# Quarter sums of the Strassen weights on VectorE, and one PSUM copy on ScalarE, in a decoder-trunk step

## The chip, the core and the metric

One Trainium2 (trn2) core runs the whole kernel as one launch. The metric is the device time of one execution in microseconds (us); three runs of the kernel before the change gave 1285.36, 1286.39 and 1287.26 us, so its median is 1286.39 us. Engines are named as in the profile: PE is TensorE's matmul, PEld its weight load, DVE is VectorE, ACT is ScalarE, POOL is GpSimd, SP is SyncE, which issues the loads.

## The reference

One inference step of a two-layer trunk, in fp32: 512 prompt tokens and 64 sample tokens (8 sequences of 8), model width 1024. Layer 0 is a gated recurrent block, layer 1 a sliding-window attention, and each is followed by a SwiGLU feed-forward block (FFN). The FFN is the part that the change touches:

```python
D_MODEL = 1024; D_FF = 2816; DEPTH = 2

def swiglu(h, w_in, w_out):
    gate, up = jnp.split(h @ w_in, 2, axis=-1)
    return (jax.nn.silu(gate) * up) @ w_out

for l in range(DEPTH):
    ...
    h = modulate(rms_norm(x, norm_g[l, 1]), sh2, sc2)
    x = x + g2[:, None, :] * swiglu(h, ffn_w_in[l], ffn_w_out[l])
```

`w_in` is 1024 x 5632 and `w_out` 2816 x 1024 in each layer.

## The kernel before

**Tiling.** The tokens stand in two halves, h = 0 and 1, of 288 columns (256 prompt and 32 sample tokens). A weight tile is 128 output columns deep over the contracted rows. To keep fp32 accuracy every operand is split into a high part (a cast to fp32r, on ACT) and a low part (the remainder, a subtraction on DVE), and a product is three matmuls of 128 x 288 per 128 rows: high by high, high by low, low by high.

**The FFN.** The first three of the 22 column tiles of each FFN are done plainly. For each of the other 19 (i = 3 to 21) the gate tile and the up tile (each 1024 x 128, loaded into a `raw` buffer of 128 x 1024) and the two token halves are taken as a 2 x 2 by 2 x 2 block product, and Strassen's form (Winograd's variant) does it with seven products of 512 rows instead of eight. A product is 12 matmuls, seven are 84. The weight operands are quarters of the gate and up tile, 128 x 512 each: r11 and r12 in the gate's buffer, r21 and r22 in the up's. The seven are called `11`, `12`, `22`, `S1`, `S2`, `S3`, `S4`: three plain quarters and four that need sums. S1 = r21 + r22; S2 needs two subtractions (r21 becomes r11 - r21, then r11 becomes r22 - r11, which is S2; the new r21 is S3); S4 = r12 - r11. All are written in place into the `raw` buffers, so each tile has four sums of 128 x 512 in fp32, 152 over both layers. `operand` (line 1204) then casts the quarter to high on ACT and subtracts on DVE for low, into a `wh` buffer; 10 `wh` and 4 `raw` buffers are shared by all weights.

**PSUM.** The seven products of a tile go to three PSUM banks (function `seven`): bank a takes `11` then `12`, bank e takes `S1` then `S4`, bank b takes `S2`, then `S3`, then `22`, each on top of what stands there. After S2 DVE adds the saved product `11` into bank b in place (`mm<-mm,ta`), and the finished sum is copied out to SBUF (`u2`, a `td` buffer). Only then may the matmuls of S3 go on in bank b. After S3 DVE adds bank b to the saved S1 product (`td<-mm,td`), and only then may `22` write on. On PE the order is S1, S2, then usually `12` and the next tile's `11`, then S3, S4, `22`.

**What follows.** silu of the gate on ACT, gate times up (on DVE for h = 0, on POOL for h = 1, `td<-td,td`), the split of the result, and after each group of 6, 6, 6 or 4 tiles eight output products of 2 x 18 (or 12) matmuls with the residual add: DVE (`x<-mm,mods,x`) and POOL (`x<-x,ta`, 128 x 32).

**What sets the order.** The code records every instruction with a cost from a small table, and a list scheduler (`schedule`) places them by priority and by the start that its cost table gives. Each engine then runs its own instructions strictly in that order. So moving an operation to another engine can change the order on all engines around it; the order is fixed when the kernel is built. Since all operations are issued from one helper line, the profile's rows carry L447 throughout, and groups are told apart by tile names: `raw` the loaded weights, `wh` split weights, `mm` PSUM banks, `ta`, `tb`, `td`, `sl` SBUF buffers, `h` the split norm output, `x` the residual stream.

The functions that the change touches, with what calls them:

Of the kernel before, what the change touches and what calls it, by code (L numbers as in the profile page):

```python
# [27 lines left out]
HC = 288  # L28
# [445 lines left out]
def trunk_kernel(ctx, tc, a):  # L474
    nc = tc.nc
    rec = Recorder(a["shadow"])
    V, S, G, T, Q = (Engine(rec, n, o) for n, o in (("DVE", nc.vector), ("ACT", nc.scalar), ("POOL", nc.gpsimd), ("PE", nc.tensor), ("SP", nc.sync)))
# [10 lines left out]
    def ps(pool=pmm, tag="mm"):  # L488
        cnt[0] += 1
        return rec.tile(pool, tag, NMM if tag == "mm" else (8 - NMM), RMM if tag == "mm" else 1, [P, 512], F32, f"{tag}{cnt[0]}")  # L490
# [509 lines left out]
    def residual(h, o, c, g, last):  # L1000
        xp, xs = x[h][:, c, 0:HP], v48(x[h][:, c, HP:HC])
        V.scalar_tensor_tensor(xp, o[:, 0:HP], mp(g, c), xp, ALU.mult, ALU.add)
        t = ta()
        V.tensor_tensor(v48(t.f[:, 0:32]), v48(o[:, HP:HC]), msam(g, c, h), ALU.mult)
        (V if g == L1 + G2 and c == KC - 1 else G).tensor_tensor(xs, xs, v48(t.f[:, 0:32]), ALU.add)
        t.done()
        if last and (g != L1 + G2 or c < KC - 1):
            square(h, c)
# [147 lines left out]
    for m in range(KC):  # L1156
# [3 lines left out]
            lambda h, o, m=m: residual(h, o, m, G1, True),  # L1160
# [8 lines left out]
    def ffn(l, g, after):  # L1169
# [34 lines left out]
        def operand(i, name, src, sums=()):  # L1204
            w = W[i, name] = whs()
            for o, p, q, op in sums:
                G.tensor_tensor(o, p, q, op)
            S.copy(w.r[:, 0:H2], src)
            V.tensor_tensor(w.r[:, H2 : 2 * H2], src, w.f[:, 0:H2], ALU.subtract)

        def steps(i):
# [8 lines left out]
            def a11():  # L1220
                operand(i, "11", views()[0])

            def a22():
                operand(i, "22", views()[3])

            def s1():
                r11, r12, r21, r22 = views()
                operand(i, "S1", r22, [(r22, r21, r22, ALU.add)])
# [36 lines left out]
        def pump(want=lambda: True):  # L1265
            while todo and (whs.live + todo[0][0] <= 2 * NHI):
                todo.popleft()[1]()
            assert want()
            load_more()

        def right(name):

            if name in ("T2", "T3", "T4"):
                return [(p.r[:, 0:HC], q.r[:, 0:HC]) for p, q in X2[int(name[1])]]
            h, c0 = {"B11": (0, 0), "B21": (0, 4), "T1": (1, 0), "B22": (1, 4)}[name]
            v = h4r(h)
            return [(v[:, k, 0, :], v[:, k, 1, :]) for k in range(c0, c0 + 4)]
# [3 lines left out]
        def seven(i, name):  # L1281

            pump(lambda: (i, name) in W)
            w = W.pop((i, name))
            bank, ops = {"11": ("a", "B11"), "12": ("a", "B21"), "S1": ("e", "T1"), "S2": ("b", "T2"), "S3": ("b", "T3"),
                         "22": ("b", "T4"), "S4": ("e", "B22")}[name]
            b = B.setdefault(i, {})
            if bank not in b:
                b[bank] = ps()
            o = b[bank][:, 0:HC]  # L1290
            first = name in ("11", "S1", "S2")
            for k, (xh, xl) in enumerate(right(ops)):
                hi, lo = [w.r[:, q + k * P : q + (k + 1) * P] for q in (0, H2)]
                T.matmul(o, hi, xh, start=first and k == 0, stop=False, skip_group_check=True)
                T.matmul(o, hi, xl, start=False, stop=False, skip_group_check=True)
                T.matmul(o, lo, xh, start=False, stop=k == 3, skip_group_check=True)
            w.done()
            pump()
            if name == "11":
                b["p1"] = ta()  # L1300
                S.copy(b["p1"].f[:, 0:HC], o)
            elif name == "S1":
                b["p5"] = td()
                S.copy(b["p5"].f[:, 0:HC], o)
            elif name == "S2":

                V.tensor_tensor(o, o, b["p1"].f[:, 0:HC], ALU.add)
                b["p1"].done()
                b["u2"] = td()
                V.tensor_copy(b["u2"].f[:, 0:HC], o)  # L1310
            elif name == "12":

                b["g"] = ta()
                S.activation(b["g"].f[:, 0:HC], o, AF.Silu)
            elif name == "S3":

                y = b["p5"].f[:, 0:HC]
                V.tensor_tensor(y, o, y, ALU.add)
            elif name == "22":

                y = b["g"].f[:, 0:HC]
                V.tensor_tensor(y, y, o, ALU.mult)
                whole(0, i, b["g"])
                del B[i]
            else:

                y, z = b["u2"].f[:, 0:HC], b["p5"].f[:, 0:HC]
                V.tensor_tensor(y, o, y, ALU.add)
                S.activation(y, y, AF.Silu)
                G.tensor_tensor(z, y, z, ALU.mult)  # L1330
                b["u2"].done()
                whole(1, i, b["p5"])

        def whole(h, f, t):
            m = mid[h][f] = (sl(F32R), sl(F32R))
            split(m[0].r[:, 0:HC], m[1].r[:, 0:HC], t.f[:, 0:HC])
            t.done()
# [20 lines left out]
        def emit():  # L1358
# [4 lines left out]
            for k in range(len(GROUPS)):  # L1363
                if k == 1 and l == 0:
                    sink_setup()
                for i in range(max(PLAIN, n_), n_ + GROUPS[k]):

                    if i == PLAIN:
                        for j, w in ((0, "11"), (1, "11"), (0, "12")):
                            seven(i + j, w)  # L1370
                    seven(i, "S1")
                    seven(i, "S2")
                    if i == PLAIN:
                        seven(i + 1, "12")
                    elif i > PLAIN + 1:
                        seven(i, "12")
                    if i > PLAIN and i + 1 < n_ + GROUPS[k]:
                        seven(i + 1, "11")
                    seven(i, "S3")
                    ada_pace(2)  # L1380
                    seven(i, "S4")
                    seven(i, "22")
# [606 lines left out]
```

## Time and profile before

| What | Value |
|---|---|
| runs | 1285.36, 1286.39, 1287.26 us |
| span of the profiled execution | 1287.3 us |
| PE busy | 1250.5 us (97%), 9532 instructions |
| DVE busy | 913.8 us (71%) |
| ACT busy | 659.3 us (51%) |
| POOL busy | 482.6 us (37%) |
| four quarter sums per tile, POOL | 152 of 128 x 512, mean 1486 and 1460 ns |
| splits of 128 x 512, DVE | 282, mean 883 ns |
| the u2 copy, DVE | 38 of 128 x 288, mean 456 ns |

The profiled execution's span, 1287.3 us, stands 0.9 us above the median of the runs and equals the slowest of them to 0.1 us; the page shows nothing around the span. A group's row reads: line, engine, operation, output <- inputs, shape, count, then total busy us and mean ns of one, then idle time of the engine before them and who ended it. A timeline row reads: start us, length us, engine, operation, number of instructions merged, and in brackets the engine's idle time before it with the releaser. The matmuls on `tb` (they belong to S2, S3 and `22`) run from 279.6 to 634.8 us in layer 0 and from 923.1 to 1244.8 us in layer 1, with output products between the groups.

### The profile page before, as it was taken

Reading aid. Unit: us, or ns where it says so; the run is one execution under the profiler, and the core shown is the slowest. Engines: PE = TensorE matmul, PEld = TensorE weight load, DVE = VectorE, ACT = ScalarE, POOL = GpSimd, SP = SyncE. Lnnn points to the kernel's source line nnn. Section 1 sums busy time; section 2 is a strip of 40 time slices with the busy share of each in tenths; the row PEclk is TensorE's granted clock in tenths of the full one; section 3 lists DMA queues with packets and bytes.
Section 4 is the critical chain, followed back from the end, with each engine's and each line's share of the span. In section 5 each row is a group of like instructions: output and inputs, shape, how many; then the busy total and the mean of one; then the engine's idle time right before and its main releaser. Section 6 shows DMA issues by size and latency. Waiting matters only on the chain.

```text
span 1287.3 us, 25427 instructions
## 1 busy us (share of the span) xinstructions
PE 1250.5 (97%) x9532; PEld 1173.3 (91%) x9532; DVE 913.8 (71%) x2161; ACT 659.3 (51%) x1470; POOL 482.6 (37%) x710
## 2 busy tenths in 40 slices
PE   7999999999999999999989999999999999999997
PEld 5788899898999999999988987899999999999997
DVE  6988785886478457646679787448965875885777
ACT  4789873753245235414466678438533542552433
POOL 3476630142354145324234435110424533642422
PEclk9999999999999999999999999899999999999998
DMA  9956454525456655554342321233241332233232
GB/s 306 326 165 217 151 164 148 169 63 184 135 152 188 192 170 164 164 180 140 107 97 48 60 75 51 68 94 111 75 123 50 99 115 80 69 107 91 67 98 74
DMA packets 223982, 165.40 MB, mean 128 GB/s; under 512 B 23758, under 2 KB 209066, under 8 KB 223827
## 3 DMA queue, kind: packets, MB, share of 16 engines
q1 hardware_dynamic: 223410, 163.45, 42.2%
q8 instruction: 75, 1.23, 0.4%
q14 instruction: 49, 0.39, 0.1%
q0 software_dynamic: 448, 0.32, 0.1%
HBM read 160.85 MB, written 4.87 MB: 129 GB/s over the span
## 4 chain that ended last, share of the span: by engine, by line
PE 76%; DVE 12%; ACT 4%; POOL 3%; issue 2%; DMA 1%; SPq 1%; ACTq 0%; POOLq 0%; DVEq 0%
PE mm L447 72%; PE ada L447 4%; DVE sl L447 4%; DVE wh L447 3%; POOL raw L447 3%; ACT wh L447 1%; DVE ta L447 1%; DVE h L447 1%; DVE td L447 1%; DVE tb L447 1%; ACT ta L447 1%; ACT L447 1%; ACT h L447 1%; SPq L447 1%; DMA wh<-in_ada_w_dram 1%
## 5 line engine op out<-in xcount | busy, mean ns | idle before, releaser
L447 PE MATMUL mm<-h,wh 128*128 128x288 f32 x4128 | 598.7, 299 | 9.2 <-ACT h L447 4.2
L447 PEld LDWEIGHTS mm<-h,wh 128*128 128x128 f32 x4128 | 563.6, 189 | 30.2 <-issue 10.7
L447 PE MATMUL mm<-sl,wh 128*128 128x288 f32 x3218 | 460.5, 296 | 0.8 <-ACT ta L447 0.8
L447 PEld LDWEIGHTS mm<-sl,wh 128*128 128x128 f32 x3218 | 436.6, 188 | 8.6 <-issue 6.7
L447 ACT CAST wh<-raw 128x512 fp32r<-128x512 f32 (+2 forms) x388 | 266.8, 710 | 301.4 <-PE mm L447 221.0
L447 DVE TENSOR_TENSOR wh<-raw,wh 128x512 fp32r<-128x512 f32 (+2 forms) x388 | 358.3, 948 | 50.5 <-ACT wh L447 46.7
L447 DVE SCALAR_TENSOR_TENSOR x<-mm,mods,x 128x256 f32<-128x256 f32 x160 | 77.1, 482 | 153.1 <-PE mm L447 152.9
L447 POOL TENSOR_TENSOR raw<-raw 128x512 f32<-128x512 f32 x76 | 110.9, 1460 | 188.1 <-DVE wh L447 187.5
L447 POOL TENSOR_TENSOR x<-x,ta 128x32 f32<-128x32 f32 x152 | 54.0, 355 | 308.7 <-DVE ta L447 308.5
L447 POOL TENSOR_TENSOR raw<-raw,raw 128x512 f32<-128x512 f32 x76 | 112.8, 1486 | 3.7
L447 PE MATMUL mm<-tb,wh 128*128 128x288 f32 (+1 forms) x488 | 89.6, 299 | 7.9 <-DVE td L447 5.4
L447 PEld LDWEIGHTS mm<-tb,wh 128*128 128x128 f32 x488 | 72.2, 188 | 12.4 <-DVE td L447 8.8
L447 POOL TENSOR_TENSOR td<-td,td 128x288 f32<-128x288 f32 x38 | 31.1, 817 | 113.7 <-ACT td L447 105.1
L447 PE MATMUL mm<-ta,wh 128*128 128x288 f32 (+1 forms) x254 | 56.0, 298 | 0.0
L447 DVE TENSOR_TENSOR td<-mm,td 128x288 f32<-128x288 f32 x76 | 33.4, 452 | 26.8 <-PE mm L447 26.5
L447 ACT ACTIVATE ta<-x 128x288 f32<-128x288 f32 x56 | 24.8, 444 | 50.9 <-POOL x L447 48.0
L447 PE MATMUL ada<-reg,cz 128*32 128x512 f32 (+1 forms) x448 | 50.3, 553 | 0.4 <-DMA reg<-in_ada_w_dram 0.2
L447 DVE TENSOR_TENSOR sl<-ta,sl 128x288 fp32r<-128x288 f32 x54 | 45.7, 849 | 2.2 <-ACT sl L447 2.0
L447 ACT COPY td<-mm 128x256 f32<-128x256 f32 (+1 forms) x102 | 33.8, 353 | 23.9 <-PE mm L447 20.8
L447 ACT ACTIVATE ta<-mm 128x288 f32<-128x288 f32 x54 | 21.4, 411 | 45.4 <-PE mm L447 44.9
L447 PEld LDWEIGHTS mm<-ta,wh 128*128 128x128 f32 x254 | 41.6, 188 | 1.7 <-ACT wh L447 0.8
L447 ACT ACTIVATE ta<-ta,stat 128x256 f32<-128x256 f32 (+2 forms) x72 | 32.3, 471 | 17.8 <-DVE stat L447 17.0
(202 smaller groups left out, 1250.4 us busy)
## 6 DMA issues: line engine op xcount, KB each, us to landing
raw<-in_ffn_w_in_dram SPq DMA_DIRECT2D x88, 512.0 KB
reg<-in_ada_w_dram SPq DMA_DIRECT2D x80, 512.0 KB
raw<-in_ffn_w_out_dram SPq DMA_DIRECT2D x48, 384.0 KB
raw<-in_rnn_w_in_dram SPq DMA_DIRECT2D x16, 512.0 KB
reg<-in_kv_ada_w_dram SPq DMA_DIRECT2D x16, 512.0 KB
wh<-in_ada_w_dram SPq DMA_DIRECT2D x24, 256.0 KB
raw<-in_rnn_w_out_dram SPq DMA_DIRECT2D x8, 512.0 KB
raw<-in_ffn_w_out_dram SPq DMA_DIRECT2D x16, 256.0 KB
```

What stands on the lines that cost most here:

```text
L447: self.rec.add(eng, lambda: getattr(obj, name)(*map(real, args), **{k: real(v) for k, v in kw.items()}), cost, outs, ins, func, lat, port, ...
```

## The change

The four sums of a Strassen tile are issued on DVE instead of POOL, and the copy of u2 out of PSUM is issued on ACT instead of DVE. Nothing else in the code is changed; the computed values are the same.

```diff
         def operand(i, name, src, sums=()):
             w = W[i, name] = whs()
             for o, p, q, op in sums:
-                G.tensor_tensor(o, p, q, op)
+                V.tensor_tensor(o, p, q, op)
             S.copy(w.r[:, 0:H2], src)
             V.tensor_tensor(w.r[:, H2 : 2 * H2], src, w.f[:, 0:H2], ALU.subtract)
...
             elif name == "S2":
                 V.tensor_tensor(o, o, b["p1"].f[:, 0:HC], ALU.add)
                 b["p1"].done()
                 b["u2"] = td()
-                V.tensor_copy(b["u2"].f[:, 0:HC], o)
+                S.copy(b["u2"].f[:, 0:HC], o)
```

The scheduler makes a new order from this. PE keeps its order up to the first Strassen tile, and outside the Strassen tiles; inside them products change places by up to 15 matmuls. Three places, on DVE and ACT.

**DVE, first Strassen tile of layer 0, before** (`wh<-raw` are splits, `mm<-mm,ta` is the add of product `11` into bank b after S2, the COPY is u2, `td<-mm,td` with mm_3940 the add after S3):

```order
L447 TENSOR_TENSOR td_3828<-td_3828,mm_3825 128x288
L447 TENSOR_TENSOR sl_3876<-td_3828,sl_3870 128x288
L447 TENSOR_TENSOR wh_3864<-raw_3400,wh_3864 128x512
L447 TENSOR_TENSOR wh_3880<-raw_3284,wh_3880 128x512
L447 TENSOR_TENSOR wh_3914<-raw_3284,wh_3914 128x512
L447 TENSOR_TENSOR wh_3931<-raw_3755,wh_3931 128x512
L447 TENSOR_TENSOR wh_3947<-raw_3894,wh_3947 128x512
L447 TENSOR_TENSOR mm_3940<-mm_3940,ta_3888 128x288
L447 COPY td_3972<-mm_3940 128x288
L447 TENSOR_TENSOR wh_3961<-raw_3755,wh_3961 128x512
L447 TENSOR_TENSOR td_3943<-mm_3940,td_3943 128x288
```

and the same stretch in the changed kernel (`raw<-raw` are sums):

```order
L447 TENSOR_TENSOR wh_3872<-raw_3755,wh_3872 128x512
L447 TENSOR_TENSOR raw_3755<-raw_3755 128x512
L447 TENSOR_TENSOR raw_3755<-raw_3500,raw_3755 128x512
L447 TENSOR_TENSOR raw_3500<-raw_3755,raw_3500 128x512
L447 TENSOR_TENSOR wh_3915<-raw_3755,wh_3915 128x512
L447 TENSOR_TENSOR raw_3500<-raw_3500 128x512
L447 TENSOR_TENSOR wh_3929<-raw_3500,wh_3929 128x512
L447 TENSOR_TENSOR wh_3936<-raw_3755,wh_3936 128x512
L447 TENSOR_TENSOR wh_3956<-raw_3500,wh_3956 128x512
L447 TENSOR_TENSOR mm_3948<-mm_3948,ta_3894 128x288
L447 TENSOR_TENSOR wh_3972<-raw_3877,wh_3972 128x512
L447 TENSOR_TENSOR wh_3997<-raw_3892,wh_3997 128x512
```

All eight sums of the first two tiles now stand ahead of the add into bank b, between the splits; the copy is gone from this queue. From the split wh_3726, which opens this stretch in both orders, to the add there are 18 instructions of 128 x 512 and two of 128 x 288.

**DVE, middle of a six-tile group of layer 1, before:**

```order
L447 TENSOR_TENSOR mm_13190<-mm_13190,ta_13116 128x288
L447 COPY td_13225<-mm_13190 128x288
L447 TENSOR_TENSOR wh_13215<-raw_12996,wh_13215 128x512
L447 TENSOR_TENSOR wh_13239<-raw_12996,wh_13239 128x512
L447 TENSOR_TENSOR wh_13246<-raw_13006,wh_13246 128x512
L447 TENSOR_TENSOR wh_13261<-raw_12996,wh_13261 128x512
L447 TENSOR_TENSOR wh_13268<-raw_13140,wh_13268 128x512
L447 TENSOR_TENSOR wh_13275<-raw_13148,wh_13275 128x512
L447 TENSOR_TENSOR td_13195<-mm_13190,td_13195 128x288
L447 TENSOR_TENSOR td_13225<-mm_13155,td_13225 128x288
```

and now:

```order
L447 TENSOR_TENSOR mm_13193<-mm_13193,ta_13123 128x288
L447 TENSOR_TENSOR wh_13222<-raw_12992,wh_13222 128x512
L447 TENSOR_TENSOR raw_12968<-raw_12968 128x512
L447 TENSOR_TENSOR wh_13251<-raw_12968,wh_13251 128x512
L447 TENSOR_TENSOR wh_13265<-raw_13106,wh_13265 128x512
L447 TENSOR_TENSOR td_13216<-mm_13193,td_13216 128x288
L447 TENSOR_TENSOR wh_13281<-raw_13130,wh_13281 128x512
L447 TENSOR_TENSOR raw_13130<-raw_13130 128x512
L447 TENSOR_TENSOR td_13234<-mm_13174,td_13234 128x288
L447 TENSOR_TENSOR raw_13130<-raw_13106,raw_13130 128x512
```

Between the add after S2 and the add after S3 (`td<-mm,td`, the first of the two) stood the copy and six splits; now three splits and one sum stand there.

**ACT, the same place, before** (COPY ta is the saved product `11`, ACTIVATE the silus, CAST wh the high parts):

```order
L447 ACTIVATE ta_13235<-mm_13093 128x288
L447 CAST wh_13239<-raw_12996 128x512
L447 CAST wh_13246<-raw_13006 128x512
L447 COPY ta_13254<-mm_13231 128x288
L447 CAST wh_13261<-raw_12996 128x512
```

and now:

```order
L447 COPY td_13216<-mm_13174 128x288
L447 CAST wh_13222<-raw_12992 128x512
L447 COPY td_13234<-mm_13193 128x288
L447 ACTIVATE ta_13242<-mm_13100 128x288
L447 CAST wh_13251<-raw_12968 128x512
L447 COPY ta_13261<-mm_13238 128x288
L447 CAST wh_13265<-raw_13106 128x512
```

The new copy (td_13234) stands behind one cast and ahead of the silu of the gate.

**DVE, first Strassen tile of layer 1, now** (raw_11955 is the first weight load of the third Strassen tile):

```order
L447 TENSOR_TENSOR wh_11969<-raw_11269,wh_11969 128x512
L447 TENSOR_TENSOR raw_11458<-raw_11458 128x512
L447 TENSOR_TENSOR wh_11985<-raw_11458,wh_11985 128x512
L447 TENSOR_TENSOR wh_11993<-raw_11819,wh_11993 128x512
L447 TENSOR_TENSOR wh_12006<-raw_11458,wh_12006 128x512
L447 TENSOR_TENSOR wh_12013<-raw_11955,wh_12013 128x512
L447 TENSOR_TENSOR mm_11987<-mm_11987,ta_11928 128x288
L447 TENSOR_TENSOR wh_12049<-raw_11995,wh_12049 128x512
L447 TENSOR_TENSOR td_12001<-mm_11987,td_12001 128x288
```

Here too all eight sums of two tiles have moved ahead of the add into bank b: from the split wh_11787, which stands at the same place in both orders, to the add there are 19 instructions of 128 x 512 and two of 128 x 288. On PE the product S2 of this tile starts 15 matmuls earlier than before, and 21 matmuls (products `12` and S4) stand between it and S3.

## The prediction

> **What bounds the kernel now.** I read the page first.
>
> ```profile
> span 1287.3 us, 25427 instructions
> PE 1250.5 (97%) x9532; PEld 1173.3 (91%) x9532; DVE 913.8 (71%) x2161; ACT 659.3 (51%) x1470; POOL 482.6 (37%) x710
> PE 76%; DVE 12%; ACT 4%; POOL 3%; issue 2%; DMA 1%; SPq 1%; ACTq 0%; POOLq 0%; DVEq 0%
> ```
>
> PE is the bound, and the change takes nothing from it. So the change can only win what PE loses to waits inside the Strassen tiles, and only lose by making new ones. Next, the stretches (length; PE, PEld, DVE, ACT, POOL busy with counts; clock; DMA share; GB/s), and PE's and PEld's waits for DVE. The last two rows below are the weight loads' waits of the windows 262 to 302 and 1000 to 1235 us.
>
> ```profile
> 262.00:296.50 34.50, 30.80 (x231) 30.32 (x229) 29.11 (x40) 16.90 (x37) 18.77 (x13) 1.00 0.28 85
> 1016.80:1039.90 23.10, 22.94 (x171) 22.48 (x170) 20.11 (x30) 12.51 (x26) 13.73 (x10) 1.00 0.29 81
> 1152.40:1235.00 82.60, 82.60 (x622) 82.42 (x623) 53.87 (x98) 30.88 (x60) 31.99 (x34) 1.00 0.29 84
> PE mm L447 <- DVE td L447: 5.4, 5, 2.6
> PEld mm L447 <- DVE td L447: 4.2, 2, 2.8
> PEld mm L447 <- DVE td L447: 2.8, 9, 0.5
> ```
>
> A matmul of a full stretch takes 82.60/622 = 0.133 us. PE idles 5.4 us for `td`; the weight loads stall longer, because a short wait disappears under the modelled ends of earlier matmuls. They are the better account: 4.2 in layer 0's first two tiles and 2.8 in layer 1's groups. PE's own rows at the places:
>
> ```profile
> 281.19 1.88 PE L447 MATMUL mm<-h,wh 128*128 128x288 f32 x13
> 284.17 1.06 PE L447 MATMUL mm<-tb,wh 128*128 128x288 f32 x6 [1.10 <-DVE td L447]
> 296.48 1.06 PE L447 MATMUL mm<-tb,wh 128*128 128x288 f32 x6 [2.60 <-DVE td L447]
> 297.38 1.35 PE L447 MATMUL mm<-sl,wh 128*128 128x288 f32 x6
> 298.52 2.94 PE L447 MATMUL mm<-h,wh 128*128 128x288 f32 x12
> 301.30 0.56 PE L447 MATMUL mm<-tb,wh 128*128 128x288 f32 x3
> 923.13 0.43 PE L447 MATMUL mm<-tb,wh 128*128 128x288 f32 x2
> 938.87 0.66 PE L447 MATMUL mm<-tb,wh 128*128 128x288 f32 x3 [1.11 <-DVE td L447]
> 1045.97 0.68 PE L447 MATMUL mm<-tb,wh 128*128 128x288 f32 x3 [0.29 <-DVE td L447]
> 297.80:301.20 3.40, 3.40 (x17) 3.40 (x16) 2.44 (x4) 0.00 (x0) 0.00 (x0) 0.51 0.39 116
> ```
>
> The last row is a window: after the 2.60 us wait the granted clock is 0.51. From 297.38 to 301.30, 18 matmuls take 3.92 us instead of 18 x 0.133 = 2.40, so 1.5 us go there. What may be won is therefore 4.2 + 1.5 in layer 0's start, 1.3 at 938.87 (1.11 idle and a late second matmul), and 2.8 in the groups: **9.8 us**, with 5.4 (the visible idle) as the least.
>
> **Why DVE is late there.** DVE and POOL around the longest wait:
>
> ```profile
> 290.23 3.52 DVE L447 TENSOR_TENSOR wh<-raw,wh 128x512 fp32r<-128x512 f32 x2 [0.66 <-ACT wh L447]
> 294.04 1.52 DVE L447 TENSOR_TENSOR sl<-ta,sl 128x288 fp32r<-128x288 f32 x1
> 295.48 0.45 DVE L447 TENSOR_TENSOR mm<-mm,ta 128x288 f32<-128x288 f32 x1
> 295.97 0.46 DVE L447 COPY td<-mm 128x288 f32<-128x288 f32 x1
> 290.21 2.98 POOL L447 TENSOR_TENSOR raw<-raw,raw 128x512 f32<-128x512 f32 x2
> 293.92 1.32 POOL L447 TENSOR_TENSOR raw<-raw 128x512 f32<-128x512 f32 x1 [0.72 <-DVE wh L447]
> ```
>
> Two splits take 3.52 us while POOL runs sums, and a small split takes 1.52 while POOL runs one more: a DVE instruction with two SBUF inputs stands still until POOL's sum is through. The add into bank b and the u2 copy come behind them, and S3 waits for the copy at 296.48.
>
> **What the change costs and saves, part by part.** The prices:
>
> ```profile
> L447 DVE TENSOR_TENSOR wh<-raw,wh 128x512 fp32r<-128x512 f32 x282 | 239.8, 883 | 38.1 <-ACT wh L447 35.1
> L447 POOL TENSOR_TENSOR raw<-raw,raw 128x512 f32<-128x512 f32 x76 | 112.8, 1486 | 3.7
> L447 POOL TENSOR_TENSOR raw<-raw 128x512 f32<-128x512 f32 x76 | 110.9, 1460 | 188.1 <-DVE wh L447 187.5
> L447 DVE COPY td<-mm 128x288 f32<-128x288 f32 x38 | 17.3, 456 | 1.0
> L447 ACT COPY td<-mm 128x288 f32<-128x288 f32 x38 | 15.2, 400 | 10.8 <-PE mm L447 10.6
> L447 POOL TENSOR_TENSOR td<-td,td 128x288 f32<-128x288 f32 x38 | 31.1, 817 | 113.7 <-ACT td L447 105.1 <-DVE td L447 8.6
> 268.68 0.68 DVE L447 TENSOR_TENSOR wh<-raw,wh 128x512 fp32r<-128x512 f32 x1
> 927.44 1.89 DVE L447 TENSOR_TENSOR wh<-raw,wh 128x512 fp32r<-128x512 f32 x3
> 257.73 3.03 DVE L447 TENSOR_TENSOR sl<-sl,sl 128x288 f32<-128x288 f32 x8
> 925.15 2.18 ACT L447 CAST wh<-raw 128x512 fp32r<-128x512 f32 x4
> ```
>
> *Sums.* POOL loses 112.8 + 110.9 = 224 us. DVE has no sum of 128 x 512 yet; the nearest is its split of the same shape and operand count. Three splits without POOL take 1.89 us, the last one 0.68 of it, so they start 0.61 apart; with POOL's lock one lasts 0.88 on average. I take 0.61: the lock's main holder is what leaves. That is 152 x 0.61 = 93 us (at most 152 x 0.88 = 134) more on DVE, beside work of PE.
>
> *Lock.* With the sums gone, 282 splits fall from 0.85 us of queue (239.8/282) toward 0.61, up to 68 us back. POOL's product `td<-td,td` and its small residual adds still lock.
>
> *Copy.* DVE loses 17 us, ACT gains 15 us at 0.40 each (its copy of the same shape and bank memory; at most the cast's 0.6 behind others). ACT was busy 12.51 of 23.10 us, so it has room.
>
> *Load per tile.* Between two adds in mid group DVE now does 11 x 0.61 plus six 128 x 288 operations (add, two more adds, a product, two splits) at 3.03/8 = 0.38: 9.0 us, and up to 0.8 for POOL's product in its way, within 84 x 0.133 = 11.2 us of PE. Before it was 20.11 of 23.10 for two tiles, about 10.1. The load hardly changes; the long single blocks go.
>
> [...]
>
> *Layer 0's start.* In the new order 18 instructions of 128 x 512 and two small ones stand from wh_3726 (the row at 268.68) to the add into bank b. 268.68 + 18 x 0.61 + 2 x 0.38 = 280.4, with up to 1 us of waits for casts 281.4, and S2 ends on PE only at 281.2. So the add ends at about 281.9 and ACT's copy (0.40 and two hops of 0.05) at 282.4, before PE needs it (281.19 + 12 x 0.133 = 282.8). The 1.10 wait goes. In the second tile from product `22`'s end: product on DVE 0.5, four 512s and two small splits 3.2, add 0.45, copy 0.5, together 4.7, against 36 matmuls, 4.8, on PE. No margin: 0 to 1 us may stay, I take 0.4. Then PE does not idle long and the 1.5 us of half clock goes too.
>
> [...] Here the drop stands 1.3 us behind that wait, so the trace speaks for the wait.
>
> *Layer 1's start.* 21 instructions stand from wh_11787 to the add:
>
> ```profile
> 912.34 1.28 DVE L447 TENSOR_TENSOR wh<-raw,wh 128x512 fp32r<-128x512 f32 x2
> ```
>
> 912.34 + 19 x 0.61 + 0.76 = 924.7, with waits 925.0, add and copy 926.0. PE starts S2 15 matmuls earlier than 923.13, at 921.1, and is through S2 and 21 more at 921.1 + 33 x 0.133 = 925.5. A wait of 0.5 (0 to 1.3) takes the place of the 1.3: 0.8 won.
>
> *Groups of layer 1.* Before, the add after S3 stood behind six splits:
>
> ```profile
> 1028.38 0.45 DVE L447 TENSOR_TENSOR mm<-mm,ta 128x288 f32<-128x288 f32 x1
> 1029.24 5.02 DVE L447 TENSOR_TENSOR wh<-raw,wh 128x512 fp32r<-128x512 f32 x6
> 1034.18 0.81 DVE L447 TENSOR_TENSOR td<-mm,td 128x288 f32<-128x288 f32 x2
> 1034.68 0.66 PE L447 MATMUL mm<-tb,wh 128*128 128x288 f32 x3
> ```
>
> Now three splits and a sum stand there, 0.38 + 4 x 0.61 = 2.8 us behind the start of the add, while S3 ends 36 matmuls, 4.8 us, after S2. DVE is idle when S3 ends, and `22` can start 0.5 us later, under S4's 1.6. S3 itself needs add and copy (1.0 us) within 24 matmuls (3.2); ACT has one cast (2.18/4 = 0.55) ahead of the copy. All 2.8 us go; I keep 0.4 back for new waits in 38 tiles.
>
> *Sum.* 3.8 + 1.5 + 0.8 + 2.4 = 8.5 us off the profiled execution: 1287.3 - 8.5 = 1278.8. It stands 0.9 above the median of the runs, so the median should come to 1286.4 - 8.5, about **1278.0 us**.
>
> **The rivals.**
>
> *A. The waits only move (no change).* S3 waits for an ACT copy that stands behind a cast, and casts wait for a free `wh` buffer. If ACT gets to the copy 2.0 us late instead of at once, S3 is 0.2 late (its margin is 3.2 - 1.0 - 0.4), and 38 tiles give back 7.6: 1286. For it: ACT already idles 10.8 us ahead of 38 copies of this shape. Against: one cast, with 1.8 us of margin.
>
> *B. DVE's queue becomes the bound (slower).* The place is the groups of six tiles: sums, splits and the adds that release PE stand in one queue, and each sum must be followed by a cast on ACT before its split can go. If such stops bring DVE's 9.8 per tile above PE's 11.2, the adds fall behind. At 0.35 us per tile, the size of the waits at 1034.68 and 1045.97 with their late second matmul, 38 tiles cost 13 us against 8.5 won: 1291. It decides from 1.4 us of stops per tile. For it: DVE waits 35.1 us for ACT's casts before its splits. Against: the order puts the casts one or two instructions ahead.
>
> *C. The start of each layer alone gains,* and the groups keep their 2.8 because the add after S3 is still late: 1280.4. It lies within the forecast's own range.
>
> **How the numbers follow.** The forecast, C with it, has 0.75, A 0.13, B 0.12. The forecast's own range is 1275.5 (all 9.8, and 1 us by chance) to 1282 (only 4.4 of it). 1286 belongs to A, so the range that holds 8 in 10 is 1275 to 1286. About 0.2%, 2.6 us, is what can be told from no change: faster than 1283.8 has the forecast's 0.75 and a little of A's, 0.77; within, most of A, 0.12; slower, 0.11.
>
> **What would show it.** POOL busy near 259 us without `raw` rows; DVE's splits of 128 x 512 near 690 ns in the mean; sums on DVE at the same; the rows of PE waiting for DVE `td` near 1 us; no half clock near 297 us. Wrong if DVE's share of a tile rises above 11 us, if PE waits for ACT `td`, or if the gain comes from other places than these three.

## The result and the profile after

The changed kernel takes 1278.99 us (median of four runs, 1278.79 to 1282.19) against 1286.83 us before (four runs on the same chip, 1285.36 to 1288.41): the medians differ by 7.84 us. The ratio on record is 0.9933, with a 95% interval of 0.9919 to 0.9947 (the medians alone give 0.9939). Forecast were 1278.0 us.

The page of the changed kernel: span, busy times, and the chain of work that ended last.

```profile
span 1277.0 us, 25350 instructions
PE 1246.2 (98%) x9532; PEld 1171.9 (92%) x9532; DVE 918.3 (72%) x2275; ACT 668.4 (52%) x1508; POOL 267.8 (21%) x558
PE 88%; DVE 7%; ACT 3%; issue 1%; POOL 0%; DMA 0%; ACTq 0%; SPq 0%; DVEq 0%; POOLq 0%
```

DVE has 114 instructions more and is busy only 4.5 us longer; POOL is busy 215 us less. In the chain PE's share went from 76% to 88%, DVE's from 12% to 7%. This execution took 1278.79 us, so 1.8 us lie around its span.

Groups of the changed kernel by line and tile (total busy us, mean ns, idle time before them):

```profile
L447 DVE TENSOR_TENSOR wh<-raw,wh 128x512 fp32r<-128x512 f32 x282 | 191.2, 694 | 46.7 <-ACT wh L447 45.3
L447 DVE TENSOR_TENSOR raw<-raw,raw 128x512 f32<-128x512 f32 x76 | 61.4, 808 | 0.9
L447 DVE TENSOR_TENSOR raw<-raw 128x512 f32<-128x512 f32 x76 | 52.1, 687 | 1.1
L447 POOL TENSOR_TENSOR td<-td,td 128x288 f32<-128x288 f32 x38 | 35.6, 936 | 476.3 <-ACT td L447 468.2 <-DVE td L447 8.1
L447 ACT COPY td<-mm 128x288 f32<-128x288 f32 x76 | 30.1, 396 | 25.5 <-DVE mm L447 16.8 <-PE mm L447 8.4
```

The splits fell from 883 to 694 ns. A sum takes as long as a split, except where POOL's product `td<-td,td`, the last long holder, is in its way: 17 of the 76 sums of the `raw<-raw,raw` group meet it and last up to 1.31 us, and the group's mean is 808 ns for that reason. The product itself became longer (817 to 936 ns).

PE's rows at the places that the prediction named, then two rows of the weight loads' waits, one for 900 to 950 and one for 950 to 1235 us. From 262 to 302 us there is no wait for `td` at all.

```profile
282.29 0.97 PE L447 MATMUL mm<-tb,wh 128*128 128x288 f32 x6
290.27 2.43 PE L447 MATMUL mm<-h,wh 128*128 128x288 f32 x17
292.54 1.04 PE L447 MATMUL mm<-tb,wh 128*128 128x288 f32 x6
919.24 1.06 PE L447 MATMUL mm<-tb,wh 128*128 128x288 f32 x6
930.03 1.06 PE L447 MATMUL mm<-tb,wh 128*128 128x288 f32 x6 [0.42 <-ACT td L447]
```

```profile
PEld mm L447 <- ACT td L447: 0.8, 2, 0.7
PEld mm L447 <- DVE sl L447: 0.2, 1, 0.2
```

The waits of 1.10 and 2.60 us at the start of layer 0 are gone; in layer 1's second tile PE waits 0.42 for ACT's copy in front of S3 where it waited 1.11 for DVE in front of `22`; of the 2.8 in the groups 0.2 is left. The operations that release PE (the add into bank b, in the groups also the add after S3, and ACT's copy), and two stretches:

```profile
280.90 0.47 DVE L447 TENSOR_TENSOR mm<-mm,ta 128x288 f32<-128x288 f32 x1
918.29 0.46 DVE L447 TENSOR_TENSOR mm<-mm,ta 128x288 f32<-128x288 f32 x1
1020.47 0.46 DVE L447 TENSOR_TENSOR mm<-mm,ta 128x288 f32<-128x288 f32 x1
1024.29 0.45 DVE L447 TENSOR_TENSOR td<-mm,td 128x288 f32<-128x288 f32 x1
1021.02 0.40 ACT L447 COPY td<-mm 128x288 f32<-128x288 f32 x1 [0.52 <-DVE mm L447]
```

```profile
262.00:290.50 28.50, 28.50 (x216) 28.49 (x215) 26.29 (x48) 15.37 (x34) 1.31 (x1) 1.00 0.35 103
1010.00:1033.10 23.10, 23.10 (x176) 23.10 (x175) 20.55 (x36) 13.32 (x30) 2.08 (x2) 1.00 0.28 80
```

From the add after S2 to the add after S3 it is now 3.82 us instead of 5.80. PE is full in both stretches, with DVE at 92% and 89%.

**Where the time went.** Every trace has 9532 matmul records, so the start of the matmul with the same number, counted from the first, can be compared between two traces (the orders differ inside the Strassen tiles, so at 2281 and 6984 it is not always the same matmul, but as many are done). The table gives, for stretches between six such numbers, how much longer (+) or shorter a stretch is than in the first profile of before. The time ahead of matmul 2097 is left out; it differs by -0.5 to +3.0 us. A layer's first two Strassen tiles are matmuls 2097 to 2281 (280.0 to 310.1 us in before) and 6848 to 6984 (920.1 to 940.0), the rest of the tiles end at 4476 (600.1) and 9222 (1240.0). One more profile of the changed kernel (e11) and two of the kernel before (e9, e10) come from the last experiments.

| Kernel | layer 0: first two tiles | rest | between | layer 1: first two tiles | rest | end |
|---|---|---|---|---|---|---|
| length before, us | 30.1 | 290.0 | 320.0 | 20.0 | 300.0 | 40.5 |
| changed | -5.6 | +0.5 | -0.7 | -0.9 | -3.3 | +0.3 |
| changed, again (e11) | -5.6 | +1.0 | -0.6 | -0.9 | -3.3 | +0.3 |
| before, second profile (e9) | -1.5 | 0.0 | -2.0 | 0.0 | +0.1 | 0.0 |
| before, third profile (e10) | 0.0 | 0.0 | -0.2 | 0.0 | 0.0 | 0.0 |
| e1, sums only | -5.6 | +0.1 | -2.4 | -1.8 | -3.2 | 0.0 |
| e2, copy only | -1.6 | +0.2 | -2.0 | -0.4 | -3.5 | 0.0 |
| e3, layer 0's first two tiles only | -4.8 | -0.2 | -1.5 | 0.0 | +0.1 | +0.1 |
| e8, all but these two | -4.4 | +0.8 | -0.7 | -0.9 | -3.6 | +0.1 |
| e6, product on VectorE too | -5.6 | +0.9 | -2.1 | -1.5 | -3.5 | +0.1 |
| e12, the same again | -5.6 | +0.3 | -0.6 | -1.5 | -3.5 | +0.2 |
| e7, short dead work on GpSimd | -5.5 | 0.0 | -0.9 | -1.5 | -3.3 | 0.0 |
| e5, dead work on VectorE | -5.6 | 0.0 | -0.3 | -1.7 | -1.2 | +0.1 |
| e4, long dead work on GpSimd | -4.7 | +1.9 | +8.4 | -1.8 | +8.3 | +0.1 |

The column "between" (attention and norms) varies by 2 us between executions of one kernel, as e9 and e10 show; nothing of the change is read from it.

**A wait that nobody forecast** costs the +0.5 and +1.0 in the rest of layer 0. Timeline rows of DVE and PE of the changed kernel:

```profile
360.76 0.21 DVE L447 TENSOR_SCALAR snk<-snk 128x1 f32<-128x1 f32 x2 [1.65 <-DMA snk<-in_attn_sinks_dram]
362.12 0.45 DVE L447 TENSOR_TENSOR td<-mm,td 128x288 f32<-128x288 f32 x1
362.62 0.66 PE L447 MATMUL mm<-tb,wh 128*128 128x288 f32 x3 [0.17 <-DVE td L447]
```

A tiny operation of layer 1's attention stands in DVE's queue, earlier than it did before, and waits 1.65 us there for its load; two splits and the add after S3 are behind it, and PE starts `22` late.

### The profile page after: what moved, and what is told of

Read it like the earlier page. It is cut to its first block, busy times and chain, and to the rows that moved or that the text cites. A ratio compares the mean times of both kernels' runs of the same rounds, so it can differ in the third digit from the quotient of the medians.

```text
span 1277.0 us, 25350 instructions
## 1 busy us (share of the span) xinstructions
PE 1246.2 (98%) x9532; PEld 1171.9 (92%) x9532; DVE 918.3 (72%) x2275; ACT 668.4 (52%) x1508; POOL 267.8 (21%) x558
## 3 DMA queue, kind: packets, MB, share of 16 engines
q8 instruction: 75, 1.23, 0.4%
## 4 chain that ended last, share of the span: by engine, by line
PE 88%; DVE 7%; ACT 3%; issue 1%; POOL 0%; DMA 0%; ACTq 0%; SPq 0%; DVEq 0%; POOLq 0%
PE mm L447 84%; PE ada L447 4%; DVE sl L447 2%; DVE ta L447 1%; DVE wh L447 1%; DVE h L447 1%; ACT ta L447 1%; ACT L447 1%; DVE tb L447 1%; ACT h L447 1%; ACT sl L447 0%; ACT wh L447 0%; ACT tb L447 0%; DVE raw L447 0%; DVE td L447 0%
## 5 line engine op out<-in xcount | busy, mean ns | idle before, releaser
L447 ACT CAST wh<-raw 128x512 fp32r<-128x512 f32 (+2 forms) x388 | 270.6, 710 | 357.3 <-PE mm L447 217.1
L447 DVE TENSOR_TENSOR wh<-raw,wh 128x512 fp32r<-128x512 f32 (+2 forms) x388 | 310.6, 812 | 59.2 <-ACT wh L447 57.1
L447 POOL TENSOR_TENSOR td<-td,td 128x288 f32<-128x288 f32 x38 | 35.6, 936 | 476.3 <-ACT td L447 468.2
L447 ACT COPY td<-mm 128x288 f32<-128x288 f32 (+2 forms) x140 | 48.7, 363 | 38.7 <-PE mm L447 18.7
L447 DVE TENSOR_TENSOR raw<-raw,raw 128x512 f32<-128x512 f32 x76 | 61.4, 808 | 0.9
L447 DVE TENSOR_TENSOR raw<-raw 128x512 f32<-128x512 f32 x76 | 52.1, 687 | 1.1
L447 DVE TENSOR_TENSOR acc<-acc,ta 128x288 f32<-128x288 f32 x54 | 24.5, 453 | 11.3 <-ACT ta L447 11.3
L447 ACT ACT_TABLE_LOAD x24 | 30.8, 1283 | 3.4 <-DMA raw<-in_c_sample_dram 3.1
```

Of the source, the lines that this page charges most:

```text
L447: self.rec.add(eng, lambda: getattr(obj, name)(*map(real, args), **{k: real(v) for k, v in kw.items()}), cost, outs, ins, func, lat, port, ...
```

## The experiments

Three explanations stood against each other. Theory 1: POOL's sums hold VectorE, and taking them away is the gain. Rival 2: the gain is the copy leaving VectorE's queue. Rival 3: POOL computes the sums slowly and so delivers operands late; the hold itself has little say. Each run is compared with runs of the kernel before that were taken beside it; e1 to e4 shared 13 such runs (median 1287.66 us), e5 to e8 seven (1287.4), e9 to e12 eleven (1288.22).

**e1: the sums on VectorE, the copy left there**

```diff
-                S.copy(b["u2"].f[:, 0:HC], o)
+                V.tensor_copy(b["u2"].f[:, 0:HC], o)
```

> The sums on VectorE, the u2 copy left on VectorE. Theory 1 (GpSimd's sums hold VectorE's two-input instructions, and so the adds that release PE come late): nearly the whole gain of 7.8 us, 1279 to 1281 us; the copy back in VectorE's queue costs at most some tenths at the tight place in layer 0's second tile. Rival 2 (the copy on VectorE is what S3 waits for, so moving it is the gain): at most half, 1283 us or more, with PE waiting for the copy at 284 and 296 us still.

Measured: 1278.54 us (1277.73 to 1282.65), ratio 0.9933, interval 0.9911 to 0.9955. The sums alone bring all of the change's gain. At layer 1's start they bring 1.8 us where the whole change brings 0.9. The copy is no part of the gain that shows in the sum, and rival 2 as the only cause is out.

**e2: the copy on ScalarE, the sums left on GpSimd**

```diff
-                V.tensor_tensor(o, p, q, op)
+                G.tensor_tensor(o, p, q, op)
```

> The u2 copy on ScalarE, the sums left on GpSimd. Theory 1: 1285.5 to 1287 us, since the add in front of the copy stays behind the held splits; the waits of 1.10 and 2.60 us in layer 0 shorten by less than 0.3 us each. Rival 2: 1283 us or less.

Measured: 1283.81 us (1281.23 to 1285.95), ratio 0.9968, interval 0.9957 to 0.9978. Theory 1 had asked for next to no gain, and missed; rival 2 had asked for 1283 us or less, and missed too. PE's row at layer 0's start, where the weight loads' two waits are 4.1 us in all, and three DVE rows from the middle of a layer 1 group:

```profile
296.07 1.07 PE L447 MATMUL mm<-tb,wh 128*128 128x288 f32 x6 [2.54 <-ACT td L447]
1012.29 0.45 DVE L447 TENSOR_TENSOR mm<-mm,ta 128x288 f32<-128x288 f32 x1
1014.09 3.65 DVE L447 TENSOR_TENSOR wh<-raw,wh 128x512 fp32r<-128x512 f32 x5 [0.75 <-ACT wh L447]
1017.65 0.81 DVE L447 TENSOR_TENSOR td<-mm,td 128x288 f32<-128x288 f32 x2
```

The two places answer differently. At layer 0's start the wait is whole and only changed its name, from DVE to ACT, since the add before the copy is as late as ever. In layer 1's groups all waits are gone and 3.5 us are won, as much as with both edits. There the add after S3 was late by only 0.1 to 0.5 us; it now starts 5.36 us after the add after S2 instead of 5.80, the length of the copy earlier, and that is enough; in e1, with the copy back and the sums in the queue, the same distance is 5.35 us. So in the groups either edit alone does it, and neither can be called the cause; at layer 0's start it is the sums.

**e3: both edits in the first two Strassen tiles of layer 0 only**

```diff
+                (V if l == 0 and i < PLAIN + 2 else G).tensor_tensor(o, p, q, op)
+                (S.copy if l == 0 and i < PLAIN + 2 else V.tensor_copy)(b["u2"].f[:, 0:HC], o)
```

> Both edits, but only for the first two Strassen tiles of layer 0. If the gains of the places add up as the prediction has them (3.8 of waits and 1.5 of half clock there): 1281 to 1282 us, and every later stage runs as before, only 5 us earlier. If the gain comes from a new order of the whole program instead: anything, with later stages changed too.

**e8: the complement, both edits everywhere but there**

```diff
+                (G if l == 0 and i < PLAIN + 2 else V).tensor_tensor(o, p, q, op)
+                (V.tensor_copy if l == 0 and i < PLAIN + 2 else S.copy)(b["u2"].f[:, 0:HC], o)
```

> The complement of e3: sums on GpSimd and the copy on VectorE in layer 0's first two Strassen tiles, both edits everywhere else. If the gains of the places add up, as my theory has it, this kernel keeps what e3 did not win: 7.8 - 3.7 to 4.5 = 3.3 to 4.2 us, so 1282.5 to 1283.6, with the waits of 1.1 and 2.5 us for td back at the start of layer 0 and none worth naming later. Rival (the stages are not independent: one place's gain is lost or taken again at the next): 1280 or less, or 1285 or more.

Measured: e3 1283.18 us (1281.37 to 1284.31), ratio 0.9963, interval 0.9947 to 0.9979; e8 1281.47 us (1280.27 to 1282.35), ratio 0.9950, interval 0.9936 to 0.9965. e3 does nothing outside its place, as forecast, though its time is 1.2 us above the forecast 1281 to 1282. But e8 wins more than the forecast 3.3 to 4.2 us: 5.9, and 4.4 of its gain stands in the very stretch where its first two tiles were left as before. Rows around S3 of the second tile, each kernel in a block of its own: before, e3, e8 (whose first row is S3 of the first tile) and the changed kernel.

```profile
292.11 1.77 PE L447 MATMUL mm<-h,wh 128*128 128x288 f32 x12
```

```profile
292.35 3.10 PE L447 MATMUL mm<-h,wh 128*128 128x288 f32 x22
295.67 0.40 ACT L447 COPY td<-mm 128x288 f32<-128x288 f32 x1 [1.11 <-DVE mm L447]
296.12 1.05 PE L447 MATMUL mm<-tb,wh 128*128 128x288 f32 x6 [0.67 <-ACT td L447]
```

```profile
285.22 1.06 PE L447 MATMUL mm<-tb,wh 128*128 128x288 f32 x6 [1.10 <-DVE td L447]
293.15 3.35 PE L447 MATMUL mm<-h,wh 128*128 128x288 f32 x24
296.43 1.92 PE L447 MATMUL ada<-reg,cz 128*32 128x512 f32 x16
296.69 0.46 DVE L447 COPY td<-mm 128x288 f32<-128x288 f32 x1
298.28 1.06 PE L447 MATMUL mm<-tb,wh 128*128 128x288 f32 x6
```

```profile
292.08 0.39 ACT L447 COPY td<-mm 128x288 f32<-128x288 f32 x1
```

e3 removes the first wait (1.1 us) and 1.9 of the second, e8 leaves the first and removes the second, 2.6: the second is counted in both. The reason is the order on PE, which an edit changes as well. Behind the end of S2, PE has 12 matmuls on `h` in front of S3 in before, 22 in e3, and in e8 24 and 16 more of the modulation (`ada`). Counted from the start of that row, the copy that S3 needs is through after 4.3 us in before, 3.7 in e3, 4.0 in e8 and, from the row at 290.27, 2.2 in the changed kernel. So in e8 the copy is hardly earlier, and the wait is gone because PE has 5.1 us of other work there; with the 12 matmuls of before (1.6 us) some 2.4 us of wait would be left, an estimate from these rows. In e3 0.6 of the 1.9 come from the copy and the rest from ten more matmuls. In the changed kernel most comes from the copy, 2.1 us, and the rest from five more matmuls. e3 and e8 also lack the half clock that followed that wait (e9 and e10, below): the six matmuls on `sl` behind S3's first six take 0.96 us in each (at 297.01 and 299.18) and 1.35 in before (297.38).

**e4: the changed kernel with dead subtractions on GpSimd**, one beside each sum, 128x512 (128x360 in layer 0), on columns that nothing reads again. Output and needed work are as in the changed kernel.

```diff
             for o, p, q, op in sums:
+                dead = mods.rearrange("p g k s -> p (g k s)")[:, 0 : 512 if l else 360]
+                G.tensor_tensor(dead, dead, dead, ALU.subtract)
                 V.tensor_tensor(o, p, q, op)
```

> The changed kernel with one more GpSimd subtraction of 128x512 (128x360 in layer 0) beside each sum, on dead columns, whose result nobody waits for. Theory 1 (the hold itself costs): splits of 128x512 on VectorE go back above 800 ns in the mean, PE waits for VectorE's adds again, 1282 to 1287 us. Rival 3 (what costs is only that a sum on GpSimd lasts 1.47 us instead of 0.69 and is late for its cast): nothing depends on these, so 1279 to 1280 us.

**e7: the same with 128x64**

```diff
+                dead = mods.rearrange("p g k s -> p (g k s)")[:, 0:64]
```

> The kernel of e4 with GpSimd's dead subtractions cut from 128x512 to 128x64: as many instructions in GpSimd's queue, beside the same sums, but each holds VectorE for a small part of the time. It tells apart what made e4 25 us slower. Theory (the time that the two engines cannot work together): within 4 us of the changed kernel, 1278 to 1283. Rival (the added instructions lead to another order of the instructions on all engines, and that order is bad, whatever the holds): 1290 or more, as in e4.

Measured: e4 1304.16 us (1303.29 to 1308.02), ratio 1.0131, interval 1.0109 to 1.0153, slower than both kernels and than every expectation. e7 1278.57 us (1277.66 to 1282.63), ratio 0.9935, interval 0.9916 to 0.9954, like the changed kernel. POOL has the same 710 instructions on both pages; so it isn't their number that costs 25 us, it is how long each lasts (from 950 to 1240 us POOL is busy 111.75 us in e4, 57.18 in e7 and 32.41 in the changed kernel). (The order of the instructions differs between the two as well; e7 shows that a new order with the added instructions costs nothing, not that e4's order is free.) How a hold reaches PE, from e4's timeline at the end of a group (POOL, DVE, ACT, PE):

```profile
1056.87 5.18 POOL L447 TENSOR_TENSOR mods<-mods 128x512 f32<-128x512 f32 x4
1058.15 1.79 DVE L447 TENSOR_TENSOR wh<-raw,wh 128x768 fp32r<-128x768 f32 x1
1059.86 1.29 DVE L447 TENSOR_TENSOR sl<-ta,sl 128x288 fp32r<-128x288 f32 x1
1061.07 1.79 DVE L447 TENSOR_TENSOR wh<-raw,wh 128x768 fp32r<-128x768 f32 x1
1062.79 0.45 DVE L447 TENSOR_TENSOR mm<-mm,ta 128x288 f32<-128x288 f32 x1
1063.33 0.40 ACT L447 COPY td<-mm 128x288 f32<-128x288 f32 x1 [4.08 <-DVE mm L447]
1063.78 1.06 PE L447 MATMUL mm<-tb,wh 128*128 128x288 f32 x6 [1.79 <-ACT td L447]
```

Four dead subtractions ran in a row. Beside them splits of 128x768 took 1.79 us (0.95 where POOL is idle) and a small split 1.29 (0.45); the add reads a PSUM bank and kept its 0.45, but started late, and the copy and S3 after it. The mean of all 128x512 splits rose only to 717 ns: what cost 25 us isn't the mean hold, it is where the holds fell. In e4's rows each of three instructions in turn loses 0.84 us whatever its own length; that is less than the 1.30 us (5.18/4) for which one subtraction lasts. Rival 3 does not explain this loss: nothing waits for these subtractions. What share late operands have in the change's own gain is not shown apart from the hold.

**e5: dead work on VectorE instead**

```diff
+                V.tensor_tensor(dead, dead, dead, ALU.max)
```

(with `dead` as in e4)

> The changed kernel with one more independent VectorE instruction (a maximum of 128x512 over dead columns; 128x360 in layer 0) beside each of the 152 sums: work that nothing needs, so the output is the same. It tests rival B's point: how much room VectorE has left in a tile. Priced as the splits of the changed kernel start, 0.60 us apart, a tile of layer 1 gets 4 x 0.6 = 2.4 us more. My theory (VectorE needs about 10.2 us of PE's 11.2 in a tile, so 1.0 us is left): the queue becomes the bound, 1.4 us over per tile, some 28 tiles of layer 1: between 10 and 40 us slower than the changed kernel, 1290 to 1320, with PE waiting for VectorE td and sl. Rival (the order of the instructions, not the sum of their times, decides; VectorE's load has no say below 100%): within 3 us of the changed kernel, 1277 to 1283, with VectorE at over 80%.

Measured: 1280.73 us (1279.25 to 1281.84), ratio 0.9946, interval 0.9930 to 0.9963. My theory asked for 1290 to 1320 us and fell. Stretches of the changed kernel and of e5 (DVE's busy time is the third):

```profile
950.00:975.00 25.00, 25.00 (x192) 25.00 (x191) 14.75 (x34) 5.09 (x8) 4.53 (x11) 1.00 0.22 66
1125.00:1150.00 25.00, 25.00 (x191) 25.00 (x191) 18.15 (x32) 13.77 (x29) 1.84 (x2) 1.00 0.35 105
```

```profile
950.00:975.00 25.00, 25.00 (x191) 25.00 (x190) 21.32 (x46) 5.09 (x8) 7.11 (x11) 1.00 0.24 70
1125.00:1150.00 25.00, 24.55 (x184) 24.07 (x182) 24.23 (x43) 13.21 (x29) 1.85 (x2) 1.00 0.32 95
```

Much of the added work went where DVE was idle, under the output products (14.75 to 21.32 us of 25), and with DVE filled to 24.23 of 25 PE lost 0.45 us there, and 2.1 us in all of layer 1's groups (-3.3 became -1.2). The rival of this expectation was right in time. What the run doesn't show is a load that must be done within its tile: dead work may be placed anywhere, a sum only between its weights and its split.

**e6 and e12: GpSimd's last product moved to VectorE too**

```diff
-                G.tensor_tensor(z, y, z, ALU.mult)
+                V.tensor_tensor(z, y, z, ALU.mult)
```

> The changed kernel with the one product that GpSimd still has in each Strassen tile (td<-td,td, 128x288, 38 of them, 936 ns each) on VectorE. It is the last holder: sums of 0.69 us last up to 1.31 where it is in the way. On VectorE it costs 38 x 0.38 = 14 us of queue, and takes away up to 38 x 0.5 of hold. My theory (after the change, holds no longer set PE's end anywhere but for the few tenths left at the three places): the same as the changed kernel to within 2 us, 1277 to 1281. Rival (GpSimd's holds still cost PE wherever they fall): 3 us or more faster, under 1276. Rival B (VectorE has no room): slower, over 1282.

> e6 again with more rounds. In e6's profile the stretch from attention's end to the last tile ended 0.7 us earlier than in the changed kernel's, with the waits of 0.4 and 0.7 us for ACT's td gone. If that is the product's hold: 0.4 to 1.0 us faster than e11 in the medians, 1277.5 to 1278.5. If GpSimd's last hold costs nothing: within 0.3 us of e11.

> The changed kernel again, in the same call as e12, so that the two can be compared by the same runs of the kernel before: ratio 0.9935 within 0.001, 1278 to 1280, and no half clock near 291.

Measured: e6 1278.15 us (1277.13 to 1279.34), ratio 0.9926, interval 0.9911 to 0.9940. With more runs of each e12 took 1278.13 us (1275.96 to 1279.92), ratio 0.9920, interval 0.9905 to 0.9936, and the changed kernel (e11) 1279.64 us (1278.39 to 1279.99), ratio 0.9930, interval 0.9915 to 0.9946. The intervals overlap. The traces agree with each other, though: in both pairs the two stretches of layer 1 together are 0.8 us shorter (-5.0 against -4.2), with PE's wait of 0.42 us for ACT at the start of layer 1 gone. I take 0.8 us, 0.06%, as likely and not shown by the times. Nor is it shown that the product's hold is the cause: e1 (-5.0) and e7 (-4.8) gain as much or nearly as much there with the product still on GpSimd. It is the fastest kernel tried, by a margin that these runs can't tell from none.

**e9 and e10: two more profiles of the kernel before**

> The kernel before once more, for a second profile of it. The waits of 1.1 and 2.5 us for td at the start of layer 0 must be there again (they follow from the order of the instructions). My theory: the half clock behind the second wait depends on how that wait lies to the chip's windows of 3.41 us, so it may or may not be there: with it the second tile's end is as late as in the first profile, without it 1.5 us earlier. Rival (the wait of 2.5 us always brings it, as the prediction had it): it is there.

> The same as e9, a third profile of the kernel before: half clock behind the second wait or not.

Measured: 1285.23 and 1289.40 us, with the same order and the same waits. PE's rows at the second wait and the stretches around it, in windows of 3.41 us. That is the step of the granted clock in the traces. In the first profile half clock starts at 21.25, 297.73, 806.32, 833.62 and 1280.77 us, 81, 149, 8 and 131 times 3.413 us apart, and lasts 3.41, 3.41, 6.83 and 3.41 us, the last time to the end; in the changed kernel it starts at 18.38, 800.03, 827.34 and 1271.07 us, 229, 8 and 130 times 3.413 apart, and lasts 3.41, 6.83 and 3.41 us and to the end; in e10 it stands at 298.11 and 806.71, again 149 times 3.413 apart. Where such steps lie in e9 and e2 no view shows: their windows are laid by an estimate of mine. e9 first (the clock is the number before the last two), then e10:

```profile
296.16 1.06 PE L447 MATMUL mm<-tb,wh 128*128 128x288 f32 x6 [2.60 <-DVE td L447]
```

```profile
291.40:294.81 3.41, 2.16 (x17) 1.92 (x15) 3.41 (x4) 1.39 (x4) 2.69 (x2) 1.00 0.13 50
294.81:298.22 3.41, 2.06 (x15) 2.06 (x16) 2.02 (x5) 0.76 (x2) 0.11 (x1) 1.00 0.02 6
297.80:301.20 3.40, 3.40 (x29) 3.18 (x31) 2.89 (x5) 1.06 (x2) 0.00 (x0) 1.00 0.40 118
```

```profile
297.01 1.05 PE L447 MATMUL mm<-tb,wh 128*128 128x288 f32 x6 [2.61 <-DVE td L447]
```

```profile
294.70:298.11 3.41, 1.10 (x8) 1.10 (x9) 2.82 (x4) 1.72 (x4) 1.07 (x1) 1.00 0.00 0
298.11:301.52 3.41, 3.41 (x16) 3.41 (x15) 2.10 (x4) 0.00 (x0) 0.00 (x0) 0.50 0.38 115
```

The same wait is followed by the half clock in e10, as in the first profile, and not in e9. In e10 PE was busy 1.10 us of the window ahead of the drop, in the first profile 1.23. No half clock (1.00 from 297.80 to 301.20) followed in e9, with 2.16 and 2.06 in its two windows, nor in e2, whose wait was 2.54 us, with 1.63 and 2.65. So the wait does not bring the half clock each time. That its position against steps of 3.41 us decides is my estimate from these four profiles; no run shows it.

## Why the prediction was right, and where it was off

**The bound and the lock: right.** PE is the bound, the gain came from its waits inside the Strassen tiles, and the sums on GpSimd are why DVE was late at layer 0's start (e1 against e2; that holds cost time at all, e4 against e7). Sums and splits follow each other 0.60 us apart on DVE (two splits in 1.29 us at 278.79, one of them 0.69), as the 0.61 taken from before. Splits at 694 ns (690 forecast; the one at 268.68 before had 0.68 us), the copy at 396 (400), DVE at 10.0 us per tile of 11.2 in the stretch at 1010 us (20.55/23.10 x 11.2; 9.0 and up to 0.8 forecast). POOL is 9 us above the forecast 259, about half of it because its product became longer.

**Layer 0's start: right, in the second tile with luck.** The add into bank b was worked out for 281.4 and came at 280.90. In the second tile two errors met: from product `22`'s end to the end of ACT's copy it took 5.4 us and not 4.7 (287.07 to 292.47), and 41 matmuls, not 36, stood in front of S3, five more being in the row at 290.27. With 36 some 0.6 us of wait would have been left, an estimate from these rows; none was, where 0.4 was kept. Without the half clock (e9 as the measure) the stretch became 4.1 us shorter (5.6 less 1.5); 3.8 were forecast.

**The half clock, 1.5 us: the step that failed.** "The trace speaks for the wait" (the one of 2.60 us in front of S3 at 296.48) was argued from one profile. Four profiles have a wait of 2.5 us or more there, and the changed kernel, e11, e3 and e8, without it, have no drop (a clock of 1.00, in e3 and e8 0.96 us for six matmuls); but the drop came in only two of the three profiles of before, with the same waits, and not in e2; it is not a cost of every execution, and the sum should have had 1.5 times a chance. What decides is not shown; PE was not idle throughout the 3.41 us ahead of the drop, but busy for 1.10 (e10) and 1.23 us (first profile).

**The base was also off.** "It stands 0.9 above the median" compared a span with whole times. The later runs have 1.8 us around the span (1283.4 in e9, of 1285.23 us), so the profiled execution of before took about 1289.1 us, an estimate from that: one of the long ones, as e10's 1289.40. For that reason the two first profiles differ by 10.3 us in span and the medians by 7.84.

**Layer 1's start: the size right, the place not.** The add was worked out for 925.0; less the 6.3 us won by then (matmul 6625 starts at 890.12 and 883.77) this is 918.7, and it came at 918.29. A wait of 0.5 was forecast for S3 of the first tile, but there PE went on at 919.24, right behind the copy, without one. The 0.42 stands at S3 of the second tile (930.03), where the add, behind a split and a sum, came at 928.88; that place was not worked out. So it is luck that the sizes agree: 0.9 us were won (0.8 forecast).

**Layer 1's groups: right in kind, too small, and not for the reason given alone.** 2.4 were forecast and 3.3 won. The 0.4 kept back "for new waits in 38 tiles" was not needed in layer 1, and the 2.8 us were nine waits from 1000 us on; from 950 us there are ten, 3.1 us in e9's profile. The six splits in front of the add after S3 did become three and a sum, but e2 shows that the copy's leaving alone would have done, and e1 the same for the sums.

**What the sum lacked.** The wait for `snk` (1.65 us on DVE at 360.76, 0.5 to 1.0 us of the stretch) was put into DVE's queue by the new order; I followed each queue at the three places and not between them. 0.3 us went at the end, of which 0.2 at one place: the last norm's matmuls at 1259.12 us waited for ACT's `ta`, a wait that the profile of before has not.

The corrected sum is 4.1 + 0.9 + 3.3 - 0.5 - 0.3 = 7.5 us, or 9.0 with the half clock; the medians gave 7.84 and, in e11's comparison, 8.58. That the forecast 8.5 lies so near is partly luck: the 0.9 us that the groups gave more and the 0.8 us of new waits nearly cancel.

**The rivals.** A (waits move to ACT's copy): 0.42 us at one place, so the sign that was to show the prediction wrong, a wait for ACT `td`, was there and was too coarse; in e4, where it was large, it came from the late add before the copy and not from casts on ACT. B (DVE's queue): its point, 1.4 us more per tile, is too low for work that may be done ahead: e5 added 4 x 0.6 = 2.4 per tile and lost 2.1 us in 16 tiles. Where it would decide for work bound to its tile was not tried. C: the groups did gain.

## What to carry to other kernels

Look for VectorE instructions with two SBUF inputs that last longer than their shape needs (here two splits in 3.52 us beside GpSimd's sums, where one takes 0.68), and for what GpSimd does at that moment; e4 was 25 us slower with a mean split of 717 ns against 694, so the price is not the mean but the longest block in front of an operation that releases TensorE. In layer 1's groups here several small causes made the same short waits, and removing either took the whole gain (3.2 us with the sums alone, 3.5 with the copy alone, 3.3 with both), so test each edit alone before giving one the credit. Where a wait is gone, look too whether other work now stands in front of it on TensorE, as in e8: then nothing became earlier. And profile a kernel more than once before a term of a microsecond or two is put into a sum.

## What the runs showed that was not expected

- The half clock starts whole multiples of 3.413 us apart in the traces (e9 and e10, above) and does not come in every execution: equal waits of 2.60 us gave 1.5 us of loss in two profiles and none in a third. In attention, too, the clock differs: 0.50 for two windows from 806 to 813 us in the first and third profile of before and 1.00 in the second, for 2 us; what decides there is not shown. Executions of before lie between 1285.23 and 1290.77 us, and that goes with the granted clock, which is on record for 31 of them: five at 0.995 took 1285.38 to 1286.06 us, the two at 0.988 1290.72 and 1290.77. The change's gain is not of that kind: at 0.993 the kernel before took 1286.76 to 1287.54 us, the changed one 1278.58 to 1279.99.
- 152 dead subtractions on GpSimd that nothing waits for cost 25 us, and the largest single loss lay far from any Strassen tile: eight of them ran in a row behind one POOL instruction in the norm before layer 1's FFN, and PE then idled 3.71 us for the norm's output `h` (e4's timeline, POOL and PE):

```profile
885.69 10.14 POOL L447 TENSOR_TENSOR mods<-mods 128x512 f32<-128x512 f32 x8
896.40 1.57 PE L447 MATMUL mm<-h,wh 128*128 128x288 f32 x5 [3.71 <-ACT h L447]
```

- DVE could be filled to 97% of a stretch of 25 us (24.23) with TensorE losing only 0.45 us in it.
